# Reading matmul columns in turn from two stretches of SBUF, with one pass of 512 columns for the high weights

## The chip, the core and the metric

The kernel runs on one core of one Trainium2 chip. A core has five engines with queues of their own: TensorE (matrix products, PE in the profile; its weight loads are shown apart as PEld), VectorE (DVE), ScalarE (ACT), GpSimd (POOL) and SyncE (SP, here only issuing DMAs). TensorE reads its operands from SBUF and writes sums to PSUM, which VectorE and ScalarE read. SBUF and PSUM have 128 partitions; a PSUM bank holds 512 float32 values per partition. The metric is the device time of one execution in microseconds, the median of several runs. A product's operands are the stationary one (the weights of the array, 128 by 128, brought by a weight load) and the moving one, whose columns stream through the array.

## The reference

A two-layer trunk over 256 tokens of width 2048. Each layer is a mixer and a gated feed-forward network, each behind an RMS norm and added to its input; the mixer is differential attention in layer 0 and a gated delta rule (a recurrent layer) in layer 1.

```python
def conv_ffn(h, w_up, conv_w, conv_b, w_down):
    u = causal_dwconv(h @ w_up, conv_w) + conv_b
    val, gate = jnp.split(u, 2, axis=-1)
    return (jax.nn.silu(gate) * val) @ w_down

def reference(x, ...):
    for i in range(DEPTH):
        h = rms_norm(x, mixer_norm[i])
        if i % N_MIXERS == 0:
            x = x + diff_attention(h, ...)
        else:
            x = x + gated_deltanet(h, ...)
        x = x + conv_ffn(rms_norm(x, ffn_norm[i]), ...)
    return x
```

All inputs are float32. Nearly all the work is `h @ w` with large weights: query, key and value projections and the output projection of the attention, the input, gate and output projections of the recurrent layer, and up and down projections (2048 to 11008, 5504 to 2048) of both feed-forward networks.

## The kernel before

Activations stand transposed: a row tile holds 128 of the 2048 features on the partitions and the 256 tokens (`T`) along the free axis. A product in full float32 is replaced by three in the faster type fp32r. Each operand is split into a high part (rounded to fp32r) and a low part (the rest), and high times high, low times high and high times low are summed. A row tile of activations holds both parts side by side: `a[:, 0, :]` is the high part (256 columns), `a[:, 1, :]` the low part.

`weights` (line 77) streams a weight chunk of four row tiles by 256 outputs, 512 KB, from HBM into `raw` on SyncE's queue (line 87); ScalarE rounds it to `whi` (line 88) and VectorE subtracts to give `wlo` (line 89). Each of the three has three buffers. The places of `whi` and `wlo` in their buffers are shifted by a number of columns that the caller gives (`place`, `dist`), so that they start at chosen distances, modulo 128 columns, from the activations.

`dense` (line 100) multiplies such chunks with the activations as the moving operand. For each row tile `k` and each of two groups `c` of 128 outputs it issues lines 115, 116 and 117, 256 columns each, into the first half of PSUM bank `c` of `ps`: high weights with high activations, low weights with high activations, high weights with low activations. `dense_tok` (line 125) does the value projection and the gate projection of the recurrent layer the other way round: activations are the stationary operand and 512 columns of weights move (lines 137 to 139). `ps` has two buffers of two banks, so that one block's sums can be read while the next block is multiplied; the other four banks are for small products.

After a block, `merge` (line 121) multiplies the sums by the inverse norm of each token on VectorE (line 123) and writes them to SBUF; it is used by the up projection, by queries and keys and by the recurrent layer's input projection, 134 times in all. Output projections go through `project` (line 237) and `add_out` (line 228), or the recurrent layer's `out` (line 659), which add the sums to the residual stream `x` (line 231, and line 247 in the last block, where the output's DMA follows). In the recurrent layer the gate columns go through `gates` (line 704).

Small products, norms and the recurrent layer's own steps are generators that `tick` (line 72) advances one step after each weight chunk, so that they stand between the large products on TensorE. They are plain float32 products, and sums of squares over partitions by fp32r products with a matrix of ones (line 225). The order of instructions on each engine is fixed when the program is built.

The order of the large products is: queries and keys, values, attention's output projection, the up and down projections, then per block of heads of the recurrent layer its input projections with the gate projection between them and the preceding block's output projection behind them, and at last the second up and down projections.

Of the kernel before, what the change touches and what calls it, by code (L numbers as in the profile page):

```python
# [8 lines left out]
F32 = mybir.dt.float32  # L9
F32R = mybir.dt.float32r  # L10
AF = mybir.ActivationFunctionType
ALU = mybir.AluOpType
# [4 lines left out]
P = 128  # L17
T = 256
D = 2048
KD = D // P  # L20
# [6 lines left out]
class Trunk:  # L27
# [72 lines left out]
    def dense(self, w, kt, acts, place, tiles=2, lead=0, dist=(45, 45)):  # L100
# [4 lines left out]
        for k0, nk in self.chunks(kt, CK, lead):  # L105
            hi, lo = self.weights(w[:, k0:k0 + nk, :], [(place - x) % P for x in dist])
            steps = [(k, c) for k in range(nk) for c in range(tiles)]
            if k0 + nk == kt:
                steps = [(k, c) for c in range(tiles) for k in range(nk)]
            for k, c in steps:  # L110
                a = acts(k0 + k)
                first, last = k0 + k == 0, k0 + k == kt - 1
                s = slice(c * P, (c + 1) * P)
                o = ps[:, c, :T]
                nc.tensor.matmul(o, hi[:, k, s], a[:, 0, :], start=first, stop=False)  # L115
                nc.tensor.matmul(o, lo[:, k, s], a[:, 0, :], start=False, stop=False)  # L116
                nc.tensor.matmul(o, hi[:, k, s], a[:, 1, :], start=False, stop=last)  # L117
            self.tick()
        return ps

    def merge(self, ps, u):

        self.nc.vector.tensor_tensor(u, ps[:, :, :T], self.rstd.unsqueeze(1).to_broadcast([P, 2, T]), ALU.mult)  # L123

    def dense_tok(self, w, kt, acts, dist):
# [4 lines left out]
        for k0, nk in self.chunks(kt, CK // 2):  # L130
            hi, lo = self.weights(w[:, k0:k0 + nk, :], 2 * ((HP + dist) % P,))
            for k in range(nk):
                a = acts(k0 + k)
                first, last = k0 + k == 0, k0 + k == kt - 1
                for c in range(2):
                    ah, al = (a[:, i, c * P:(c + 1) * P] for i in range(2))
                    nc.tensor.matmul(ps[:, c, :], ah, hi[:, k, :], start=first, stop=False)  # L137
                    nc.tensor.matmul(ps[:, c, :], ah, lo[:, k, :], start=False, stop=False)  # L138
                    nc.tensor.matmul(ps[:, c, :], al, hi[:, k, :], start=False, stop=last)  # L139
# [87 lines left out]

    def add_out(self, blk, ps, done):

        x = self.x[:, 2 * blk:2 * blk + 2, :]  # L230
        self.nc.vector.tensor_tensor(x, ps[:, :, :T], x, ALU.add)
# [5 lines left out]
    def project(self, w, kt, acts, place, done, final=False):  # L237

        n = KD // 2
        for b in range(n):  # L240
# [4 lines left out]
            for c in range(2):  # L245
                k = 2 * b + c
                self.nc.vector.tensor_tensor(self.x[:, k, :], ps[:, c, :T], self.x[:, k, :], ALU.add)
# [456 lines left out]
    def gates(self, gd, pg, nv, gp, ident, triu, res):  # L704
# [7 lines left out]
        nc.vector.tensor_tensor(lin, pg[:, 0, :T], self.rstd, ALU.mult)  # L712
# [45 lines left out]
NH = 8  # L758
# [11 lines left out]
def _layout(inputs):  # L770
# [30 lines left out]
    for t, n in ((0, P), (1, T)):  # L801
# [9 lines left out]
        for i in range(2)]  # L811
    out = {
# [3 lines left out]
        "w_v": blocks(x["diff_w_qkv"][0], KD, [[(2 * NH * T + T * h, 2 * T)] for h in range(0, NH, 2)]),  # L816
# [8 lines left out]
        "w_z": blocks(wi, KD, gz),  # L825
# [77 lines left out]
```

## Time and profile before

| | |
|---|---|
| median of 3 runs | 2648.79 us (2647.02 to 2650.22) |
| the profiled execution, first to last instruction | 2646.8 us |
| mean granted TensorE clock | 0.999 |
| weight DMAs (the queue's total) | 475.58 MB in 134064 packets |
| mean DMA traffic | 182 GB/s |

In the profile, a row of a group gives the source line, the engine, the operation, the names `out<-in`, the shapes, the count, then busy time in us and the mean of one in ns, then the time that the engine stood idle just before them and what ended it. Rows of the timeline give start and length in us, and the count of equal instructions merged. Matrix products overlap: the time from one start to the next, not the length of a row, is what each takes of TensorE. A plain float32 product appears as two records, an fp32r product as one.

Stages by the time in which their weights are loaded: attention up to 402 us, first up projection to 871, first down projection to 1105, recurrent layer to 1940, second up projection to 2409, second down projection to the end.

### The profile page before, as it was taken

The page shows a single profiled execution, that of the slowest core. Times are in us where ns is not written, and L with a number is a line of the kernel's source. Part 1 is how long each engine was busy: PE and PEld are TensorE (multiplying, and loading weights), DVE is VectorE, ACT ScalarE, POOL GpSimd, SP SyncE. Part 2 cuts the span into 40 slices and gives each one's busy share as a digit, 9 for nine tenths or more (in the row PEclk, how much of TensorE's full clock was granted, in tenths as well). Part 3 has the DMA queues.
Part 4 walks back from the last instruction along what each step waited for, and adds up shares of the span by engine and source line. Part 5 has one row for each costly group of instructions (what it writes and reads, how often), then busy time and mean ns, then how long its engine had stood idle before and what let it go on. Part 6 is the DMA issues. An engine that isn't in the chain of part 4 may idle for free.

```text
span 2646.8 us, 53675 instructions
## 1 busy us (share of the span) xinstructions
PE 2630.0 (99%) x22352; PEld 2568.2 (97%) x22352; DVE 1843.3 (70%) x2719; ACT 1452.6 (55%) x1994; POOL 112.9 (4%) x221
## 2 busy tenths in 40 slices
PE   8999999999999999999999999999999999999999
PEld 8998899999999999999989989989999999999999
DVE  7776567777777555589787788688677777775444
ACT  6655555555555444485674674574555555554333
POOL 0000000000000000021011021021000000000000
PEclk9999999999999999999999999999999999999999
DMA  5555566665656666555455455455455666666665
GB/s 201 173 176 167 166 192 194 193 196 193 194 195 193 196 192 195 186 161 188 132 167 168 150 168 169 152 169 174 152 194 193 196 193 193 195 194 197 202 201 166
DMA packets 135460, 481.62 MB, mean 182 GB/s; under 512 B 15408, under 2 KB 18480, under 8 KB 135216
## 3 DMA queue, kind: packets, MB, share of 16 engines
q1 hardware_dynamic: 134064, 475.58, 56.5%
q8 instruction: 175, 2.87, 0.4%
q10 hardware_dynamic: 1152, 2.61, 0.3%
q14 instruction: 69, 0.57, 0.1%
HBM read 476.03 MB, written 2.10 MB: 181 GB/s over the span
## 4 chain that ended last, share of the span: by engine, by line
PE 94%; ACT 2%; DVE 2%; issue 1%; DMA 1%; POOL 0%; SPq 0%; DVEq 0%; ACTq 0%
PE ps L115 27%; PE ps L117 27%; PE ps L116 27%; PE ps L138 3%; PE ps L139 3%; PE ps L137 3%; PE mp L607 2%; DVE wlo L89 1%; ACT whi L88 1%; PE mp L225 1%; DVE cv L206 0%; DMA raw<-w_in 0%; PE mp L577 0%; PE mp L571 0%; ACT L454 0%
## 5 line engine op out<-in xcount | busy, mean ns | idle before, releaser
L89 DVE TENSOR_TENSOR wlo<-raw,whi 128x1024 fp32r<-128x1024 f32 (+2 forms) x909 | 1105.6, 1217 | 640.9 <-ACT whi L88 638.6
L88 ACT CAST whi<-raw 128x1024 fp32r<-128x1024 f32 (+2 forms) x909 | 948.1, 1044 | 999.4 <-PE ps L117 835.4
L115 PE MATMUL ps<-h,whi 128*128 128x256 f32 x4304 | 1192.5, 277 | 9.0 <-ACT h L151 5.7
L116 PE MATMUL ps<-h,wlo 128*128 128x256 f32 x4304 | 1192.3, 277 | 3.1 <-DVE wlo L89 3.1
L117 PE MATMUL ps<-h,whi 128*128 128x256 f32 x4304 | 1192.2, 277 | 0.0
L115 PEld LDWEIGHTS ps<-h,whi 128*128 128x128 f32 x4304 | 809.3, 188 | 11.2 <-ACT h L151 5.7
L116 PEld LDWEIGHTS ps<-h,wlo 128*128 128x128 f32 x4304 | 809.8, 188 | 5.6 <-DVE wlo L89 4.0
L117 PEld LDWEIGHTS ps<-h,whi 128*128 128x128 f32 x4304 | 809.8, 188 | 0.7
L115 PE MATMUL ps<-ac,whi 128*128 128x256 f32 x1632 | 450.4, 276 | 0.0
L116 PE MATMUL ps<-ac,wlo 128*128 128x256 f32 x1632 | 450.3, 276 | 0.0
L117 PE MATMUL ps<-ac,whi 128*128 128x256 f32 x1632 | 450.2, 276 | 0.0
L115 PEld LDWEIGHTS ps<-ac,whi 128*128 128x128 f32 x1632 | 306.2, 188 | 0.0
L116 PEld LDWEIGHTS ps<-ac,wlo 128*128 128x128 f32 x1632 | 306.2, 188 | 0.0
L117 PEld LDWEIGHTS ps<-ac,whi 128*128 128x128 f32 x1632 | 306.2, 188 | 0.0
L137 PE MATMUL ps<-whi,h 128*128 128x512 f32 x384 | 150.1, 391 | 0.0
L138 PE MATMUL ps<-wlo,h 128*128 128x512 f32 x384 | 149.7, 390 | 0.2
L139 PE MATMUL ps<-whi,h 128*128 128x512 f32 x384 | 149.2, 388 | 0.0
L115 PE MATMUL ps<-oc,whi 128*128 128x256 f32 x512 | 143.1, 280 | 0.0
L117 PE MATMUL ps<-oc,whi 128*128 128x256 f32 x512 | 142.9, 279 | 0.0
L116 PE MATMUL ps<-oc,wlo 128*128 128x256 f32 x512 | 142.8, 279 | 0.0
L206 DVE SCALAR_TENSOR_TENSOR cv<-u,fcols,cv 128x255 f32<-128x255 f32 (+1 forms) x344 | 142.8, 477 | 0.0
L123 DVE TENSOR_TENSOR u<-ps,rstd 128x512 f32<-128x512 f32 x118 | 81.4, 690 | 38.4 <-PE ps L117 37.7
(202 smaller groups left out, 2180.2 us busy)
## 6 DMA issues: line engine op xcount, KB each, us to landing
raw<-w_up SPq DMA_DIRECT2D x344, 512.0 KB, 4.3
raw<-w_down SPq DMA_DIRECT2D x160, 512.0 KB, 4.1
raw<-w_in SPq DMA_DIRECT2D x128, 512.0 KB, 4.3
raw<-w_z SPq DMA_DIRECT2D x64, 512.0 KB, 3.7
raw<-w_out SPq DMA_DIRECT2D x64, 512.0 KB, 3.6
raw<-w_qk SPq DMA_DIRECT2D x63, 512.0 KB, 4.1
raw<-w_v SPq DMA_DIRECT2D x32, 512.0 KB, 3.6
raw<-w_o SPq DMA_DIRECT2D x32, 512.0 KB, 4.4
```

What stands on the lines that cost most here:

```text
L88: nc.scalar.copy(hi, raw)
L89: nc.vector.tensor_tensor(lo, raw, hi.bitcast(F32), ALU.subtract)
L115: nc.tensor.matmul(o, hi[:, k, s], a[:, 0, :], start=first, stop=False)
L116: nc.tensor.matmul(o, lo[:, k, s], a[:, 0, :], start=False, stop=False)
L117: nc.tensor.matmul(o, hi[:, k, s], a[:, 1, :], start=False, stop=last)
L123: self.nc.vector.tensor_tensor(u, ps[:, :, :T], self.rstd.unsqueeze(1).to_broadcast([P, 2, T]), ALU.mult)
L137: nc.tensor.matmul(ps[:, c, :], ah, hi[:, k, :], start=first, stop=False)
L138: nc.tensor.matmul(ps[:, c, :], ah, lo[:, k, :], start=False, stop=False)
L139: nc.tensor.matmul(ps[:, c, :], al, hi[:, k, :], start=False, stop=last)
L206: nc.vector.scalar_tensor_tensor(out[:, j:], u[:, :T - j], taps[n - 1 - j], out[:, j:], ALU.mult, ALU.add)
L225: last = self.nc.tensor.matmul(out, self.onesr, p[:, j], start=i + j == 0, stop=i + j == n)
L607: nc.tensor.matmul(p[:, v, :], l(v), r[:, v, :], start=i == 0, stop=i == len(terms) - 1)
```

## The change

Moving operands are read in another order. `turns` gives a view of a stretch of columns in which the first and the second half are read in turn: column 0, column 128, column 1, column 129 and so on. In `dense`, the high weights now run over the high and low activations in one pass of 512 columns, which fills a whole PSUM bank (sums of the high part in the first half, of the low part in the second); the low weights run over the high activations and are added to the first half. In `dense_tok` the three products stay, and the weights' columns are read in turn; the arrays `w_v` and `w_z` are permuted on the host, so that their sums come out in natural order. In `dense` the sums come out interleaved, and their readers undo it: `halves` gives the two halves of a bank in natural order. `merge` copies the second half to SBUF on ScalarE, adds it to the first half on VectorE and multiplies by the norm; the residual addition becomes two additions, one for each half (`add_x`). The sums of `gates` go through `merge` too.

```diff
-                o = ps[:, c, :T]
-                nc.tensor.matmul(o, hi[:, k, s], a[:, 0, :], start=first, stop=False)
-                nc.tensor.matmul(o, lo[:, k, s], a[:, 0, :], start=False, stop=False)
-                nc.tensor.matmul(o, hi[:, k, s], a[:, 1, :], start=False, stop=last)
+                nc.tensor.matmul(ps[:, c, :], hi[:, k, s], self.turns(a), start=first, stop=False)
+                nc.tensor.matmul(ps[:, c, :T], lo[:, k, s], self.turns(a[:, :1, :]), start=False, stop=last)
...
+    def turns(self, a):
+
+        return a.rearrange("p i (q j) -> p i j q", q=2)
+
+    def halves(self, ps):
+
+        return [ps[:, :, i * T:(i + 1) * T].rearrange("p c (j q) -> p c q j", q=2) for i in range(2)]
+
     def merge(self, ps, u):
-        self.nc.vector.tensor_tensor(u, ps[:, :, :T], self.rstd.unsqueeze(1).to_broadcast([P, 2, T]), ALU.mult)
+        nc = self.nc
+        n = u.shape[1]
+        main, small = self.halves(ps[:, :n])
+        t = self.sp.tile([P, 2, T], F32, tag="mt", name="mt", bufs=1)[:, :n]
+        v = "p c (q j) -> p c q j"
+        nc.scalar.copy(t.rearrange(v, q=2), small)
+        nc.vector.tensor_tensor(u.rearrange(v, q=2), main, t.rearrange(v, q=2), ALU.add)
+        nc.vector.tensor_tensor(u, u, self.rstd.unsqueeze(1).to_broadcast([P, n, T]), ALU.mult)
...
-                    nc.tensor.matmul(ps[:, c, :], ah, hi[:, k, :], start=first, stop=False)
-                    nc.tensor.matmul(ps[:, c, :], ah, lo[:, k, :], start=False, stop=False)
-                    nc.tensor.matmul(ps[:, c, :], al, hi[:, k, :], start=False, stop=last)
+                    wh, wl = self.turns(hi[:, k:k + 1, :]), self.turns(lo[:, k:k + 1, :])
+                    nc.tensor.matmul(ps[:, c, :], ah, wh, start=first, stop=False)
+                    nc.tensor.matmul(ps[:, c, :], ah, wl, start=False, stop=False)
+                    nc.tensor.matmul(ps[:, c, :], al, wh, start=False, stop=last)
...
+    def add_x(self, k, n, ps):
+        x = self.x[:, k:k + n, :].rearrange("p c (q j) -> p c q j", q=2)
+        for part in self.halves(ps):
+            self.nc.vector.tensor_tensor(x, part, x, ALU.add)
+
     def add_out(self, blk, ps, done):
-        x = self.x[:, 2 * blk:2 * blk + 2, :]
-        self.nc.vector.tensor_tensor(x, ps[:, :, :T], x, ALU.add)
+        self.add_x(2 * blk, 2, ps)
...
-        nc.vector.tensor_tensor(lin, pg[:, 0, :T], self.rstd, ALU.mult)
+        self.merge(pg, lin.unsqueeze(1))
...
+    def turned(w):
+        return w.reshape(*w.shape[:-1], T, 2).swapaxes(-1, -2).reshape(w.shape)
```

More of the change, by code (lines that the diff above doesn't have):

```diff
@@ L824, in _layout @@
         "w_in": blocks(wi, KD, gin),
[L825 removed]
+        "w_z": turned(blocks(wi, KD, gz)),
         "w_out": go.reshape(NB * (D // T), P, 2 * HB, T),
```

4 lines of the change are left out of this document (2 added, 2 removed).

## The prediction

> **What bounds the kernel now.** I read the page first: busy times, chain, costliest groups.
>
> ```profile
> span 2646.8 us, 53675 instructions
> PE 2630.0 (99%) x22352; PEld 2568.2 (97%) x22352; DVE 1843.3 (70%) x2719; ACT 1452.6 (55%) x1994; POOL 112.9 (4%) x221
> PE 94%; ACT 2%; DVE 2%; issue 1%; DMA 1%; POOL 0%; SPq 0%; DVEq 0%; ACTq 0%
> L115 PE MATMUL ps<-h,whi 128*128 128x256 f32 x4304 | 1192.5, 277 | 9.0 <-ACT h L151 5.7
> L115 PE MATMUL ps<-ac,whi 128*128 128x256 f32 x1632 | 450.4, 276 | 0.0
> L115 PE MATMUL ps<-oc,whi 128*128 128x256 f32 x512 | 143.1, 280 | 0.0
> L137 PE MATMUL ps<-whi,h 128*128 128x512 f32 x384 | 150.1, 391 | 0.0
> ```
>
> TensorE's own stream is 94% of the chain and hardly ever idle. The mean of one product (277 ns) is a latency of overlapping products; what one costs is the step from start to start. The view by stretches gives it where nothing but lines 115 to 117 runs (500 to 800 us), and shows the stages; columns are length, then busy time and count of each engine, granted clock, DMA share, GB/s.
>
> ```profile
> core 0: us, PE busy (x) PEld busy (x) DVE busy (x) ACT busy (x) POOL busy (x), PEclk, DMA share, GB/s
> 500.00:800.00 300.00, 300.00 (x2650) 300.00 (x2649) 214.90 (x306) 163.66 (x222) 0.00 (x0) 1.00 0.60 194
> 403.00:872.00 469.00, 469.00 (x4139) 468.95 (x4138) 335.04 (x477) 257.29 (x349) 0.00 (x0) 1.00 0.61 194
> 1107.00:1420.00 313.00, 311.64 (x2440) 292.04 (x2440) 266.41 (x481) 205.57 (x284) 50.42 (x103) 1.00 0.53 168
> 1420.00:1834.00 414.00, 413.29 (x3569) 391.86 (x3569) 326.75 (x538) 245.43 (x336) 59.97 (x112) 1.00 0.51 163
> 1200.00:1210.00 10.00, 10.00 (x45) 8.26 (x44) 9.55 (x22) 5.64 (x7) 0.00 (x0) 1.00 0.67 208
> ```
>
> 300 us / 2650 = 113.2 ns per product of 256 columns, at a granted clock of 1.00. Next the timeline of TensorE, for products of 512 columns, plain fp32 products of 256 (line 372), and the small fp32r products of line 225.
>
> ```profile
> 255.62 0.39 PE L138 MATMUL ps<-wlo,h 128*128 128x512 f32 x1
> ...
> 265.40 0.39 PE L139 MATMUL ps<-whi,h 128*128 128x512 f32 x1
> 265.62 0.59 PE L372 MATMUL mp<-aT,v 128*128 128x256 f32 x2
> 266.05 0.38 PE L373 MATMUL mp<-aT,v 128*128 128x128 f32 x2
> 266.27 0.38 PE L372 MATMUL mp<-aT,v 128*128 128x256 f32 x1
> ...
> 273.37 0.64 PE L225 MATMUL mp<-sqp,onesr 128*128 128x256 f32 x4
> 273.84 0.39 PE L138 MATMUL ps<-wlo,h 128*128 128x512 f32 x1
> ```
>
> From 255.62 to 265.40 stand 44 products, so 43 steps: 9.78/43 = 227.4 ns for 512 columns. That is twice 113.2 to within 0.5%, with one weight load in either. So the step is set by columns (0.442 ns each) and holds no visible price per product or per load. A plain fp32 record of 256 columns takes (266.05 - 265.62)/2 = 215 ns, 0.84 ns a column: less than twice 0.442. So the array can go a little faster than the fast products go; at half the column rate some 5% of loss is gone. I read this as a limit on how fast contiguous four-byte columns reach the array, since a slower array clock would have stretched both kinds alike. This reading carries the forecast.
>
> **The change, part by part.** Lines 115 to 117 run 4304 + 1632 + 512 = 6448 times, one set for each row tile and 128 outputs, so now cost 3 x 113.2 = 339.6 ns a set. Lines 137 to 139 run 3 x 384 = 1152 products.
>
> *Joining the two passes of the high weights.* Three loads become two; columns stay 768 a set. As the step is set by columns, this alone is worth nothing: bounds 0 and, if a hidden price of 2 ns sat in each product (rounding of the two steps above), 6448 x 2 ns = 13 us. I take 0. The load of the next high weights must now fit beside the 256-column pass; it did fit within 113.2 ns, so this can hold that pass at 113 ns and no higher.
>
> *Columns in turn from two stretches 128 columns apart.* No row shows such a read; every moving operand is contiguous now. If it lifts the limit, a fast column costs half a plain fp32 column: 512 columns 215 ns, 256 columns 107.5 ns, or up to 113 if the load holds it. I take 215 + 109 = 324 ns. A set then saves 339.6 - 324 = 15.6 ns, times 6448 = 101 us; lines 137 to 139 save (227.4 - 215) x 1152 = 14 us. Together 115 us. Lower bound on the saving: none (the limit stays), or a loss (rivals). Upper bound: line 373 takes (266.27 - 266.05)/2 = 110 ns for 128 columns, twice which is 5 more than 215; so 5 ns of a plain fp32 record may be a price per product, which the fast ones don't show. Without it 512 columns take 210 and 256 take 105: savings of 24.6 ns x 6448 + 17.4 ns x 1152 = 179 us. The starts are given to 0.01 us, an error as large as these 5 ns, so I put the bound halfway, 147 us.
>
> *More work to read the sums.* Rows by line:
>
> ```profile
> L123 DVE TENSOR_TENSOR u<-ps,rstd 128x512 f32<-128x512 f32 x118 | 81.4, 690 | 38.4 <-PE ps L117 37.7
> L123 DVE TENSOR_TENSOR qkr<-ps,rstd 128x512 f32<-128x512 f32 x16 | 11.0, 689 | 1.3 <-PE ps L117 0.6
> L231 DVE TENSOR_TENSOR x<-ps,x 128x512 f32<-128x512 f32 x55 | 37.8, 687 | 23.5 <-PE ps L117 23.3
> L612 ACT COPY w<-mp 128x512 f32<-128x512 f32 x8 | 4.7, 588 | 13.6 <-PE mp L607 13.6
> L88 ACT CAST whi<-raw 128x1024 fp32r<-128x1024 f32 x887 | 931.0, 1051 | 963.3 <-PE ps L117 803.2 <-PE ps L139 65.8 <-ACT cv L204 50.3
> ```
>
> Each of the 134 merges (118 + 16, and a narrow one for the gates) gains a ScalarE copy (588 ns, line 612) and a VectorE addition (690 ns): 79 and 92 us in all. Each of 55 residual additions becomes two: 38 us. The readers now step over every second PSUM element; no row prices that. Bounds: nothing, or double (each such instruction 0.69 us more). I take nothing: the nearest rows are lines 123 and 231, which read as many PSUM elements and already go over two banks.
>
> Is it covered? A feed-forward block in the stage 403 to 872 holds 335.04/43 = 7.79 us of VectorE and 257.29/43 = 5.98 us of ScalarE in 10.9 us. After: 8.48 and 6.57 in 32 x 324 ns = 10.37 us, so 82% and 63%; with doubled reads 9.17 us, 88%, still under. The merge's addition waits for its copy, and the copy may stand behind one weight cast (1051 ns); behind the addition on VectorE stand the next low-weight subtraction and the convolution. ScalarE's casts wait mostly for TensorE to free a buffer (803.2 us): the weights are ahead by the three buffers, so about 2 us of delay inside a block stays hidden. The sums have two buffers, and the next block covers ten microseconds.
>
> In the first recurrent block (1107 to 1420) it is tight: VectorE 266.41 of 313 us and, around the inversion, 9.55 of 10. Fifteen merges fall there (10 us more VectorE), and TensorE's own time falls by about 13 us. 277 of 300 us is 92% as a mean, so I charge these 10 us in full as exposed; in the later blocks (326.75 of 414) nothing. At the end, the last addition comes twice:
>
> ```profile
> 2642.99 0.42 DVE x L247
> 2643.42 0.33 DVEq L899
> ```
>
> which adds 0.42 us, and at the start the first wide pass needs the low half of the activations as well, about 0.5 us. Costs: 11 us.
>
> **Sum.** 2646.8 - 115 + 11 = 2542.8 us of span. The runs' median, 2648.79, lies 2.0 us above the profiled span, which I keep: 2545 us.
>
> **The rivals.**
>
> *R1, the limit is per column in any order.* Then the turned read changes nothing, joining passes gives nothing, and the 11 us of costs remain: 2648.8 + 11 = 2660; with VectorE well covered, 2650. For it: the loss is so exactly proportional to columns that it could belong to fast products as such, fed from anywhere. Against: the plain fp32 row. This is the case in which the change doesn't do what it says.
>
> *R2, changing stretch at every column halves the reader.* One mechanism: if the reader fetches a group of neighbouring columns at once and holds only one group, each turned column needs its own fetch. It decides as soon as a fetch costs more than one column's time. Price: the plain fp32 pace, 0.84 ns a column: a set 645 ns (430 + 215), 305 more, times 6448 = 1969 us, and 1152 x (430 - 227) = 234 us: 2648.8 + 2203 = about 4850 us. Against it: nothing in the rows; a contiguous read never tests it. The Trainium skill, page SBUF — State Buffer, section Specifications, says that lines are 16 bytes and that full bandwidth needs at least two hits per line, each move to a new line paying. By that rule turned columns hit each line once before leaving it, and R2 would hold; no run here shows it, and contiguous columns, with four hits per line, already lose.
>
> *R3, the gain is taken back by collisions of two reads.* The code places weights and activations at chosen distances (arguments 45, 27, 15), so the relative place of weight load and moving columns matters. Line 225, which is not placed so, takes (273.84 - 273.37)/4 = 117.5 ns, 4.3 more than 113.2. The turned read walks both stretches at half speed while the distances stay as they were. If that costs 4.3 ns per 256 columns everywhere: (3 x 6448 + 2 x 1152) x 4.3 = 93 us, and the gain shrinks to 115 - 93 - 11 = 11: 2638 us.
>
> **How the numbers follow.** Chances: forecast 0.64, R1 0.16, R2 0.12, R3 0.08. A measurement of this kernel tells about 0.2% (5 us) from no change. The forecast and R3 are faster: 0.72. R1 splits into within 0.2% (0.05) and slower (0.11); R2 is slower: 0.12, so 0.23. The forecast's own range runs from 2648.8 - 147 = 2502 (costs hidden) to 2590 (the load holding the short pass at 113 ns, 26 us, and some 19 us from doubled PSUM reads in the recurrent blocks). The range goes from there over R3 and R1 to 2665 and leaves out R2 and the far tail.
>
> **What would show it.** In the feed-forward stage each set should step 322 to 328 ns, the wide pass 215 and the short one 108 to 113, and products of lines 137 to 139 about 215; TensorE idle as now. Under R1 227 and 113 stand; under R2 near 430 and 215; under R3 steps between, differing by line with the placement. Idle time of TensorE behind the low weights between 1107 and 1420 would show VectorE as the bound. The forecast is wrong if the wide pass still steps 227.

## The result, and the profile after

The changed kernel takes 2613.5 us (median of 4 runs, 2612.4 to 2618.3) against 2649.4 us before (4 runs): a ratio of 0.9872, interval 0.9858 to 0.9886. It is 36 us faster. The forecast was 104 us faster (2545), so the direction was right and the size was not, by 68 us.

First the page of the changed kernel: span, busy times, TensorE's granted clock in 40 slices, the chain that ended last, and four of the costliest groups.

```profile
span 2611.1 us, 41169 instructions
PE 2557.8 (98%) x15904; PEld 2328.6 (89%) x15904; DVE 1945.4 (75%) x2911; ACT 1510.2 (58%) x2119; POOL 107.2 (4%) x221
PEclk9999999999999999999989999999799999999999
PE 95%; ACT 2%; DVE 1%; DMA 1%; issue 1%; SPq 0%; ACTq 0%; DVEq 0%
L114 PE MATMUL ps<-h,whi 128*128 128x512 f32 x4304 | 1427.0, 385 | 19.1 <-ACT zt L704 9.7
L115 PE MATMUL ps<-h,wlo 128*128 128x256 f32 x4304 | 1182.7, 275 | 2.2 <-DVE wlo L89 2.2
L245 DVE TENSOR_TENSOR x<-ps,x 128x512 f32<-128x512 f32 (+1 forms) x114 | 77.0, 676 | 16.5 <-PE ps L115 15.4
L136 DVE TENSOR_TENSOR u<-u,rstd 128x512 f32<-128x512 f32 x118 | 81.7, 692 | 3.3
```

Products fell from 22352 to 15904, which is the 6448 joined passes. VectorE gained 102 us and ScalarE 58. TensorE is 98% busy and not 99%, and its clock, full in all slices before, has two slices below 9. The residual additions (L245) now step over every second PSUM element. The 110 of them of full size take 685 ns where contiguous ones took 687; the 676 of the row takes in four of half the size.

Next the stretches of the changed kernel: one inside the first up projection, where only the dense products run, and then the recurrent layer in five stretches. That layer begins at 1053 us, its last block ends at 1919, and the inner marks are where its four bursts of token-major products (L151 to L153) begin. The last two rows lie inside the third of the five.

```profile
500.00:800.00 300.00, 300.00 (x1834) 275.89 (x1833) 238.31 (x343) 184.58 (x258) 0.00 (x0) 1.00 0.60 201
...
1053.00:1127.00 74.00, 73.31 (x449) 66.65 (x448) 58.71 (x109) 50.68 (x74) 7.50 (x16) 1.00 0.58 188
1127.00:1270.00 143.00, 142.07 (x988) 127.03 (x987) 122.00 (x208) 87.59 (x120) 26.18 (x46) 1.00 0.56 178
1270.00:1500.00 230.00, 216.16 (x1458) 194.63 (x1457) 180.43 (x310) 136.16 (x196) 23.74 (x53) 0.96 0.45 145
1500.00:1702.00 202.00, 198.76 (x1345) 179.68 (x1343) 167.91 (x281) 119.97 (x165) 26.05 (x53) 0.98 0.52 169
1702.00:1919.00 217.00, 197.95 (x1262) 177.04 (x1262) 161.79 (x281) 118.02 (x174) 23.52 (x50) 0.91 0.41 135
...
1343.00:1356.00 13.00, 8.78 (x28) 7.26 (x29) 7.43 (x19) 4.41 (x7) 2.30 (x8) 0.51 0.00 1
1356.00:1366.00 10.00, 10.00 (x63) 9.22 (x62) 8.46 (x16) 4.68 (x5) 0.00 (x0) 1.00 0.41 131
```

The same five stretches of the kernel before:

```profile
1094.00:1174.00 80.00, 78.79 (x668) 77.47 (x667) 61.34 (x118) 57.48 (x83) 17.51 (x30) 1.00 0.53 169
1174.00:1337.00 163.00, 162.85 (x1361) 152.63 (x1361) 136.75 (x241) 104.47 (x148) 21.39 (x49) 1.00 0.50 157
1337.00:1546.00 209.00, 208.60 (x1759) 198.16 (x1758) 165.02 (x273) 127.04 (x176) 31.07 (x59) 1.00 0.51 163
1546.00:1752.00 206.00, 205.69 (x1744) 195.12 (x1743) 161.06 (x268) 124.16 (x168) 28.49 (x53) 1.00 0.51 164
1752.00:1929.00 177.00, 177.00 (x1516) 167.72 (x1515) 141.05 (x230) 94.21 (x131) 14.28 (x28) 1.00 0.51 169
```

In the up projection 1834 products are 917 sets, 300 / 917 = 327 ns each; from start to start in the trace it is 327.5 (218.3 for the wide pass, 109.2 for the short one), of 339.6 before. That is what the change was for, and it is there. The table has every stage, each from the first load of its weights to that of the next; here and below stage times are differences of two starts in the trace, us.

| stage | before | after | difference |
|---|---|---|---|
| attention: qk, v, o projections | 389.4 | 374.5 | -14.9 |
| first up and down projection | 703.4 | 677.5 | -25.9 |
| recurrent layer | 835.1 | 865.7 | +30.6 |
| second up and down projection | 716.8 | 691.9 | -24.9 |

Outside the recurrent layer the change gains 66 us. Inside it 31 go again, though the sets and the token-major products are shorter there too. The two lists of stretches show where: the first two gain 26 us together (217 of 243), the fourth 4, the third loses 21, the last 40. In those two TensorE stands idle 14 and 19 us and its mean clock is 0.96 and 0.91. Over the layer its records show half clock for 65 us, in pieces of 3.4 to 17 us; before there were none.

The timeline of TensorE in the third stretch has one such place (columns: start, duration, engine, line, operation, and in brackets the idle time before it and what ended it).

```profile
1340.31 0.36 PE L492 MATMUL mp<-grow,sel 128*128 128x256 f32 x1 [1.00 <-DVE d L495]
1343.98 0.77 PE L514 MATMUL mp<-cv 128*128 128x128 f32 x2 [3.32 <-DVE cv L507]
...
1346.68 1.06 PE L604 MATMUL mp<-con,cv 128*128 128x128 f32 x4
1350.98 0.79 PE L114 MATMUL ps<-h,whi 128*128 128x512 f32 x1 [3.24 <-ACT zt L704]
```

Small products of the recurrence (L492, L514, L515, L604) stand next to each other with no dense product between them. TensorE waits for VectorE and then for ScalarE, in these rows twice more than 3 us, and around these gaps it goes at half clock (0.51 in the window from 1343 to 1356, 1.00 in the next): the wide pass at 1350.98 takes 0.79 us as a record where the mean is 0.385. What put the small products there, and why VectorE is late, is what the experiments below take apart.

### The profile page after: what moved, and what is told of

Same layout as the page of the kernel before. It is cut to its first block, busy times and chain, and to the rows that moved or that the text cites. A ratio compares the mean times of both kernels' runs of the same rounds, so it can differ in the third digit from the quotient of the medians.

```text
span 2611.1 us, 41169 instructions
## 1 busy us (share of the span) xinstructions
PE 2557.8 (98%) x15904; PEld 2328.6 (89%) x15904; DVE 1945.4 (75%) x2911; ACT 1510.2 (58%) x2119; POOL 107.2 (4%) x221
## 3 DMA queue, kind: packets, MB, share of 16 engines
q10 hardware_dynamic: 1152, 2.61, 0.3%
## 4 chain that ended last, share of the span: by engine, by line
PE 95%; ACT 2%; DVE 1%; DMA 1%; issue 1%; SPq 0%; ACTq 0%; DVEq 0%
PE ps L114 54%; PE ps L115 27%; PE ps L151 3%; PE ps L153 3%; PE ps L152 3%; PE mp L625 2%; PE mp L239 1%; PE mp L515 1%; ACT whi L88 0%; DMA raw<-w_in 0%; PE mp L595 0%; PE mp L589 0%; DVE wlo L89 0%; PE mp L604 0%; DMA raw<-w_qk 0%
## 5 line engine op out<-in xcount | busy, mean ns | idle before, releaser
L89 DVE TENSOR_TENSOR wlo<-raw,whi 128x1024 fp32r<-128x1024 f32 (+2 forms) x909 | 1104.2, 1215 | 535.4 <-ACT whi L88 521.8
L114 PE MATMUL ps<-h,whi 128*128 128x512 f32 x4304 | 1427.0, 385 | 19.1 <-ACT zt L704 9.7
L115 PE MATMUL ps<-h,wlo 128*128 128x256 f32 x4304 | 1182.7, 275 | 2.2 <-DVE wlo L89 2.2
L114 PEld LDWEIGHTS ps<-h,whi 128*128 128x128 f32 x4304 | 818.8, 190 | 135.0 <-ACT zt L704 10.8
L115 PEld LDWEIGHTS ps<-h,wlo 128*128 128x128 f32 x4304 | 831.4, 193 | 5.1 <-DVE wlo L89 3.6
L114 PE MATMUL ps<-ac,whi 128*128 128x512 f32 x1632 | 535.1, 382 | 0.0
L115 PE MATMUL ps<-ac,wlo 128*128 128x256 f32 x1632 | 444.8, 273 | 0.0
L114 PEld LDWEIGHTS ps<-ac,whi 128*128 128x128 f32 x1632 | 308.4, 189 | 43.1 <-issue 0.2
L115 PEld LDWEIGHTS ps<-ac,wlo 128*128 128x128 f32 x1632 | 313.3, 192 | 0.1
L114 PE MATMUL ps<-oc,whi 128*128 128x512 f32 x512 | 171.0, 387 | 0.9 <-DVE oc L673 0.9
L151 PE MATMUL ps<-whi,h 128*128 128x512 f32 x384 | 146.2, 381 | 0.9 <-ACT whi L88 0.9
L153 PE MATMUL ps<-whi,h 128*128 128x512 f32 x384 | 145.9, 380 | 0.0
L115 PE MATMUL ps<-oc,wlo 128*128 128x256 f32 x512 | 141.1, 276 | 0.0
L114 PEld LDWEIGHTS ps<-oc,whi 128*128 128x128 f32 x512 | 98.2, 192 | 15.1 <-DVE oc L673 1.3
L115 PEld LDWEIGHTS ps<-oc,wlo 128*128 128x128 f32 x512 | 99.5, 194 | 0.1
L218 ACT ACTIVATE cv<-u,fcols 128x256 f32<-128x256 f32 x172 | 93.9, 593 | 0.6 <-DVE u L136 0.5
L245 DVE TENSOR_TENSOR x<-ps,x 128x512 f32<-128x512 f32 (+1 forms) x114 | 77.0, 676 | 16.5 <-PE ps L115 15.4
L220 DVE SCALAR_TENSOR_TENSOR cv<-u,cols,cv 128x255 f32<-128x255 f32 (+2 forms) x192 | 84.5, 477 | 1.9 <-ACT cv L216 1.8
L136 DVE TENSOR_TENSOR u<-u,rstd 128x512 f32<-128x512 f32 x118 | 81.7, 692 | 3.3
```

Of the source, the lines that this page charges most:

```text
L89: nc.vector.tensor_tensor(lo, raw, hi.bitcast(F32), ALU.subtract)
L114: nc.tensor.matmul(ps[:, c, :], hi[:, k, s], self.turns(a), start=first, stop=False)
L115: nc.tensor.matmul(ps[:, c, :T], lo[:, k, s], self.turns(a[:, :1, :]), start=False, stop=last)
L136: nc.vector.tensor_tensor(u, u, self.rstd.unsqueeze(1).to_broadcast([P, n, T]), ALU.mult)
L151: nc.tensor.matmul(ps[:, c, :], ah, wh, start=first, stop=False)
L153: nc.tensor.matmul(ps[:, c, :], al, wh, start=False, stop=last)
```

## The experiments

### One part at a time

*turn_only* keeps three passes and turns the columns of each; there is one read of the sums.

```diff
-                nc.tensor.matmul(ps[:, c, :], hi[:, k, s], self.turns(a), start=first, stop=False)
-                nc.tensor.matmul(ps[:, c, :T], lo[:, k, s], self.turns(a[:, :1, :]), start=False, stop=last)
+                o = ps[:, c, :T]
+                ah, al = self.turns(a[:, 0:1, :]), self.turns(a[:, 1:2, :])
+                nc.tensor.matmul(o, hi[:, k, s], ah, start=first, stop=False)
+                nc.tensor.matmul(o, lo[:, k, s], ah, start=False, stop=False)
+                nc.tensor.matmul(o, hi[:, k, s], al, start=False, stop=last)
```

> Three passes of 256 columns as before, but every large product reads its moving columns in turn; one VectorE read of the sums, as before. Theory A (the gain is all in the turned read, the loss of the changed kernel is in what joining brought into the recurrent layer): a set of three steps 3 x 109.2 = 327.6 ns, a 512-column product 216 to 219; the recurrent layer, 835 us before and 866 us in the changed kernel, takes about 809; total 2649 - 80 - 10 = about 2559 us. Rival B (faster large products alone uncover the recurrent layer's own latencies): the recurrent layer stays near 866 and the total near 2613. Rival C (the passes are faster only where joined): 113 ns a pass, total 2640 to 2650.

*join_only* keeps the joined pass and reads all columns in order (w_v and w_z not permuted).

```diff
     def turns(self, a):
-        return a.rearrange("p i (q j) -> p i j q", q=2)
+        return a
```

> One pass of 512 columns for the high weights, all columns contiguous; copies and additions as in the changed kernel. Theory A: 227 + 113 = 340 ns a set, feed-forward up stages 468 us as before, and a recurrent layer that loses as in the changed kernel (some 40 to 57 us over its product time): total 2680 to 2705 us. Rival C (joining brings the rate): 328 ns a set, total near 2613. Rival B: with slow products nothing is uncovered, the recurrent layer stays near 835 and the total near 2655.

Measured: turn_only 2602.1 us (ratio 0.9834, 0.9819 to 0.9848), 44 us faster than before and 11 faster than the whole change. join_only 2771.0 us (1.047, 1.0454 to 1.0486). The same stretch of the up projection, turn_only first, then join_only:

```profile
500.00:800.00 300.00, 300.00 (x2689) 300.00 (x2688) 216.81 (x309) 165.91 (x225) 0.00 (x0) 1.00 0.66 197
```

```profile
500.00:800.00 300.00, 300.00 (x1733) 262.10 (x1732) 227.60 (x325) 173.68 (x245) 0.00 (x0) 1.00 0.59 190
```

A turned pass of 256 columns steps 111.7 ns from start to start (300 / 2689 = 111.6), and not the 109.2 expected, so no total that was expected for turn_only is met. A set is 335, 4.6 less than before: 6448 x 4.6 + 1152 x 12.4 = 44 us, which is the whole gain of this kernel. In join_only a set takes 347 ns from start to start (230.9 + 115.8), 7 more than three separate passes, and 353 in the second up projection. So joining is worth about nothing only in the forecast: with contiguous columns it costs, with turned ones it gains 335 - 327.5 = 7.5 ns a set. In the recurrent layer turn_only takes 819.8 us, 15 less than before: turning alone loses nothing there. join_only takes 907.6 us there, 72 more than before, of which its longer sets are 11 to 21 (1552 sets in that layer, 7 to 14 ns each). So the loss in that layer comes with joining, whether columns are turned or not.

### What a column costs, and what a pass

*probe* is the kernel before with a pattern of its own in each block of the up and down projections: the columns in q stretches, d columns apart, taken in turn; in the second up projection with the joined pass.

```diff
+    def turn(self, a, q, d):
+        if d == 0:
+            return a
+        return a.rearrange("p (g q j) -> p g j q", q=q, j=d)
```

> Steps of the large products by the way in which columns are read. The kernel before with its three passes, but the first up projection changes its reading order every five blocks: contiguous; two stretches 128, 64, 32, 16, 8, 4, 2 columns apart; four stretches 64 apart. The second up projection uses the joined form: contiguous; 128 apart; 256 apart with 128 for the low weights; 64; 32; high turned and low contiguous; high contiguous and low turned; four stretches; eight. The first down projection (turned) and the second (contiguous) change the place of the weights every block. The sums stay in the order of reading and the second half of a joined bank is not read, so these terms are left out. Theory E (any second stretch lifts the limit): 113 contiguous, 109 for all distances down to 4. Rival F (the two reads must lie in other 64-byte pieces): 109 at 16 and above, 113 at 8 and below. Rival G (a full round of the weights' placement matters): steps that follow the place of the weights by 4 ns and more, turned or not. For the joined pass: 218.4 at 128 as in the changed kernel, 216 at 256 as for the products that move weights.

Windows of *probe*, three passes: two stretches 128, 4 and 2 columns apart, then four stretches 64 apart. After these, joined sets: contiguous; 128 apart; only the wide pass turned. (A window of some 40 us counts two or three products that only overlap its edges; steps in the text are from start to start. *probe* and *widths* ran once each, for these steps alone.)

```profile
458.00:508.00 50.00, 50.00 (x451) 50.00 (x450) 36.86 (x53) 27.74 (x40) 0.00 (x0) 1.00 0.63 196
726.00:776.00 50.00, 50.00 (x451) 50.00 (x450) 36.85 (x53) 27.63 (x40) 0.00 (x0) 1.00 0.58 198
790.00:830.00 40.00, 40.00 (x355) 40.00 (x354) 29.02 (x43) 22.14 (x31) 0.00 (x0) 1.00 0.60 194
834.00:870.00 36.00, 36.00 (x266) 36.00 (x265) 21.62 (x31) 16.42 (x24) 0.00 (x0) 1.00 0.52 165
...
1965.00:1995.00 30.00, 30.00 (x172) 26.38 (x171) 20.58 (x30) 15.76 (x21) 0.00 (x0) 1.00 0.59 184
2010.00:2045.00 35.00, 35.00 (x215) 32.21 (x215) 26.00 (x38) 19.75 (x28) 0.00 (x0) 1.00 0.60 201
2210.00:2255.00 45.00, 45.00 (x270) 41.34 (x269) 32.28 (x46) 24.70 (x34) 0.00 (x0) 1.00 0.56 196
```

| columns | 256 alone, ns | joined set, ns (wide + short) |
|---|---|---|
| contiguous | 113.3 | 353.3 (231.8 + 121.5) |
| two stretches, 128 to 4 apart | 111.7 | 327.5 (218.3 + 109.2), 32 to 256 apart |
| two stretches, 2 apart | 113.3 | not run |
| wide pass turned, short one contiguous | | 335.6 (215.8 + 119.8) |
| wide pass contiguous, short one turned | | 340.0 (231.7 + 108.3) |
| four stretches | 136.7 | 390.0 (278.2 + 111.8) |

Two columns apart, a turned pair lies within 16 bytes, and there is no gain; from four columns (16 bytes) apart there is all of it. Two stretches in turn help; four lose. The down projections of the same kernel vary where the weights lie against the activations. Turned, all eight placements step 111.66 to 111.67 ns; contiguous, they step 113.4 to 123.3. So the place of the weights costs a contiguous read up to 10 ns and a turned read nothing; I take it for a collision with the weight load, which no run shows apart. By the same reading the joined contiguous passes of join_only stand in a bad place, a worse one in its second feed-forward stage (353 ns) than in its first (347); other places were not tried for them.

*widths* is the kernel before with all three passes of the up projections at one width per five blocks, turned in the first and contiguous in the second.

```diff
+                    n = max(wide, T) if first else wide
+                    x = a.rearrange("p i t -> p (i t)")[:, :n]
+                    if turned:
+                        x = x.rearrange("p (q j) -> p j q", q=2)
```

> The kernel before, but in both up projections the three products of a set run over 64, 128, 192, 224, 256, 288, 320, 384 or 512 columns, changing every five blocks (the first row tile of a block over at least 256); first stage turned, second contiguous. Widths below 256 leave columns out, the others read more of the same. Theory H (a weight load holds 111.7 ns and sets the step of a turned pass of 256): turned 111.7 at all widths up to 256, then about 121, 135, 162 and 216. Rival I (a fixed price of about 5 ns a product): turned 33, 60, 86, 98, 112, 125, 138, 165, 218. Contiguous above 256: 0.442 ns a column plus what the place of the weights adds: 128, 142, 170, 227 or more.

Its windows for 64, 128, 224, 256, 288 and 384 turned columns:

```profile
420.00:490.00 70.00, 70.00 (x330) 70.00 (x329) 27.28 (x40) 21.81 (x29) 0.00 (x0) 0.50 0.32 105
510.00:590.00 80.00, 80.00 (x377) 80.00 (x376) 32.09 (x44) 22.97 (x32) 0.00 (x0) 0.50 0.31 100
...
660.00:708.00 48.00, 48.00 (x432) 48.00 (x432) 34.88 (x51) 26.27 (x37) 0.00 (x0) 1.00 0.62 197
715.00:760.00 45.00, 45.00 (x405) 45.00 (x404) 32.09 (x47) 25.01 (x34) 0.00 (x0) 1.00 0.63 197
770.00:820.00 50.00, 50.00 (x410) 50.00 (x409) 33.39 (x46) 24.79 (x35) 0.00 (x0) 1.00 0.57 180
895.00:960.00 65.00, 65.00 (x402) 65.00 (x401) 32.78 (x46) 24.80 (x34) 0.00 (x0) 1.00 0.42 138
```

From 192 to 256 columns a product steps 111.7 ns whatever its width, as theory H expected, then 122.5 at 288, 135.8 at 320, 162.5 at 384 and 215.8 at 512. These widths lie on one line, 0.417 ns a column and 2.5 ns, which meets 111.7 near 260 columns: above it the columns set the step, below it a floor for each product that does not depend on them. At half clock the floor is 213.3 ns, for 64 and 128 columns alike, so it goes with TensorE's clock. I take it for the weight load, of which each product has one. No run here shows that: the load rows are busy all the time at 288 and 384 columns too, where the columns set the step. Contiguous passes follow the same floor (112 at 192 and 224 columns) and above it cost more: 133.3, 148.4 and 180.0 at 288, 320 and 384. Before the change, 113.2 ns was a column price just above this floor.

### The recurrent layer: the reads

*one_read* is the changed kernel with the second read of the sums taken out: the copy and the addition in `merge` and the second residual addition.

```diff
-        nc.scalar.copy(t.rearrange(v, q=2), small)
-        nc.vector.tensor_tensor(u.rearrange(v, q=2), main, t.rearrange(v, q=2), ALU.add)
-        nc.vector.tensor_tensor(u, u, self.rstd.unsqueeze(1).to_broadcast([P, n, T]), ALU.mult)
+        r = self.rstd.rearrange("p (q j) -> p q j", q=2).unsqueeze(1).to_broadcast([P, n, 2, P])
+        nc.vector.tensor_tensor(u.rearrange(v, q=2), main, r, ALU.mult)
```

> The changed kernel, but the sums of high weights with low activations are computed and never read: this leaves out one of the three terms, with its ScalarE copies and its second VectorE additions. Rival D (the recurrent layer of the changed kernel is late because VectorE and ScalarE have more to do): its 57 us come back, total about 2557. Theory A in the form that the fixed order of the small steps costs the time: most of it stays where small steps stand in rows with no large product between them (the last block above all), total 2575 to 2600.

*mix* is a full version: three turned passes and one read in the recurrent layer, joined and turned elsewhere.

```diff
+                if not self.joined:
+                    ...
+                    continue
...
+            self.joined = False
...
+            self.joined = True
```

> The changed kernel, with three turned passes and one read of the sums in the recurrent layer alone. Theory A: attention and feed-forward as in the changed kernel, the recurrent layer about 809 instead of 866 us, total about 2556 us. Rival B: the recurrent layer near 866, total near 2613.

*mix_reads* is mix with the third pass of the recurrent layer written to the second half of the bank, so that the sums are read twice as in the changed kernel.

```diff
-                    nc.tensor.matmul(o, hi[:, k, s], al, start=False, stop=last)
+                    nc.tensor.matmul(ps[:, c, T:], hi[:, k, s], al, start=False, stop=last)
```

> As mix (recurrent layer with three turned passes), but there the low activations' pass goes to the second half of the bank, and the sums are read twice, with the copy and the additions of the changed kernel. Rival D (the copies and additions cost the time): the recurrent layer, 823 us in mix and 866 in the changed kernel, rises to 840 or more, total 2590 or more. Theory A in the form that the fixed order of the small steps costs it: the extra reads alone cost under 8 us there, total 2571 to 2579.

*mix_out* is mix with the last projection of the recurrent layer (w_out) joined too.

```diff
+                    self.joined = True
...
+                    self.joined = False
```

> As mix, but the output projection of the recurrent layer is joined too (512 sets at 327.5 instead of 335 ns: 3.8 us). If joining as such is harmless where the small steps keep large products between them: total 2567 us, 4 below mix. If any joined product in that layer brings the loss back: 2580 or more.

Measured: one_read 2592.5 us (0.9797, 0.9782 to 0.9812); mix 2570.8 (0.9716, 0.97 to 0.9732); mix_reads 2579.2 (0.974, 0.9725 to 0.9754); mix_out 2574.6 (0.9723, 0.9707 to 0.9739). The recurrent layers take 846.9, 822.7, 832.9 and 825.0 us. So mix gains everything that the change gains outside the layer, and 12 us inside it, where the change loses 31. It is 43 us faster than the changed kernel and the fastest full version here; mix_out is the same within the noise. The 809 us that were expected for the layer of mix again took a turned pass at 109.2 ns. mix_out was to gain 4 us on mix or lose 9 and more, and does neither, so it decides little. The last three stretches of mix:

```profile
1288.00:1493.00 205.00, 204.78 (x1770) 196.18 (x1769) 165.01 (x282) 126.75 (x178) 31.91 (x56) 1.00 0.53 165
1493.00:1702.00 209.00, 204.44 (x1757) 194.66 (x1757) 164.46 (x276) 128.24 (x178) 28.89 (x61) 1.00 0.52 163
1702.00:1876.00 174.00, 173.89 (x1523) 166.52 (x1522) 140.58 (x231) 94.67 (x132) 14.14 (x28) 1.00 0.55 172
```

With the reads taken out of the changed kernel its layer is 19 us shorter (865.7 to 846.9); with them put into mix it is 10 longer, between the two outcomes expected. But one_read is still 24 us behind mix, with the same work on VectorE and ScalarE in that layer, and its clock stands at half for 48 us. The reads are not all of it.

### The recurrent layer: the order

The order of TensorE's instructions is fixed when a kernel is built. Set side by side, before and turn_only, whose passes have the same shapes, have the same order, with dense products between the small steps of the recurrence. The changed kernel and join_only, with joined passes, share another: at the end of three blocks, and through almost all of the last, the small steps stand in rows with no dense product between. The longest such row of the changed kernel has 276 records and spans 33.6 us; in the kernel before the longest spans 2.7. mix has dense products there. one_read has an order of its own, with its longest row, 33.1 us, in the last block too. Three kernels fix the order of TensorE's products. They leave the order on VectorE and ScalarE to the build, and in the traces it comes out differently in each, so what is called the price of the order or of the reads below holds with what the build made of these engines.

*pinned* is the changed kernel with each group of small steps held behind the last dense product issued before it in the code, and the next dense product behind the small steps.

```diff
+        with self.tc.issue_after(self.big):
+            self.steps()
...
+                if self.pinned and self.small is not None:
+                    self.tc.add_manual_dep(f.ins, self.small.name, NOSYNC)
```

> The changed kernel with the same instructions; only TensorE's order in the recurrent layer is fixed to the order in which the code issues them, with a chunk of large products between any two steps of the small ones. If the loss there comes from the order (small steps in rows with nothing large between, TensorE idle and its clock halved behind): the recurrent layer falls from 866 us to 815 to 830, no stretch at half clock, total 2560 to 2578. If it comes from the work of copies and additions or from the faster products as such: it stays at 845 or more, total 2590 or more.

*same_order* is the changed kernel with TensorE's products of the recurrent layer in the order of mix; *same_order_one* does that to one_read. (`ORDER` is that order, listed.)

```diff
+            rank = [k for a, n in ORDER for k in range(a, a + n)]
+            for a, b in zip(rank, rank[1:]):
+                self.tc.add_manual_dep(items[b][0], items[a][-1].name, NOSYNC)
```

> The changed kernel, instruction for instruction; in the recurrent layer TensorE's products are queued in the order that the build gave to mix, so that a joined set stands where mix has its three passes. If the loss of joining there is the order that the build makes for it: the recurrent layer takes 811 to 825 us instead of 866, with no stretch at half clock, total 2556 to 2572. If it is the copies and additions: 840 or more, total 2588 or more. If faster products as such uncover the small steps: 850 or more.

> As same_order, but the sums of high weights with low activations are computed and never read (one of the three terms is left out, with its copies and additions). If the order is the cause, about 811 us in the recurrent layer (mix's 823 less 1552 sets at 7.5 ns), total 2552 to 2560; against same_order it gives the price of the extra reads under one and the same order of products, between 0 and 10 us.

Measured: pinned 2720.3 us (1.0278, 1.0261 to 1.0296), the layer 970.2: the other way from what was expected. The order of the code puts the steps of the block inversion behind each other where nothing hides them, as the waits of TensorE in *pinned* show (what waits, for what: us in all, times, longest):

```profile
PE mp L591 <- DVE tcc L572: 56.6, 4, 15.0
```

It is a worse order, so it tells nothing of what is wrong with the build's, but it shows the range: 849 to 970 us with identical instructions. same_order takes 2595.7 us (0.9806, 0.979 to 0.9822), the layer 849.4, which is the outcome expected if copies and additions cost it, though 16 us below the changed kernel; same_order_one 2571.1 (0.9714, 0.97 to 0.9729), the layer 823.6 where 811 was expected. The last three stretches of same_order, 21 us of the first of them, two waits of its TensorE in the layer, and the same stretches of same_order_one:

```profile
1289.00:1513.00 224.00, 207.83 (x1384) 185.07 (x1383) 175.68 (x303) 137.31 (x195) 26.28 (x63) 0.98 0.49 153
1513.00:1727.00 214.00, 204.04 (x1373) 183.38 (x1372) 173.21 (x290) 132.06 (x184) 27.51 (x54) 0.98 0.50 156
1727.00:1902.00 175.00, 171.14 (x1192) 153.84 (x1192) 147.78 (x243) 97.50 (x134) 14.18 (x28) 1.00 0.54 169
...
1385.00:1406.00 21.00, 13.41 (x97) 11.79 (x97) 20.22 (x34) 6.96 (x7) 2.10 (x6) 0.94 0.59 194
```

```profile
PE mp L571 <- DVE tcc L552: 9.6, 3, 7.0
PE ps L116 <- DVE wlo L90: 6.5, 5, 3.0
```

```profile
1289.00:1496.00 207.00, 203.27 (x1382) 183.48 (x1381) 165.15 (x283) 127.06 (x180) 33.18 (x59) 0.99 0.53 163
1496.00:1705.00 209.00, 202.97 (x1369) 181.61 (x1368) 162.31 (x274) 127.05 (x176) 25.25 (x58) 0.99 0.51 162
1705.00:1877.00 172.00, 169.80 (x1187) 152.87 (x1186) 138.25 (x227) 94.17 (x132) 13.97 (x28) 1.00 0.53 172
```

The last stretch is 217 us in the build's order and 175 in mix's, with the reads in both: that stretch is the order's. The first two go the other way (217 and 236 us): the build's order takes dense products early that are missing as cover at the end, so the net price is 865.7 - 849.4 = 16 us. The third stretch is 224 us with the reads and 207 without, in one order of TensorE: that one is the reads'. There TensorE waits 7 us for VectorE's part of the block inversion (tcc), which comes late behind residual additions and low weights: VectorE is busy 20.2 of the 21 us up to there. Elsewhere it waits for the low weights (wlo).

| recurrent layer, us | one read | two reads |
|---|---|---|
| three passes, order of mix | 822.7 | 832.9 (own order) |
| joined, order of mix | 823.6 | 849.4 |
| joined, the build's order | 846.9 | 865.7 |

In the last column the order of TensorE costs 16 us; in the middle row the reads cost 26, where 0 to 10 were expected. The 23 us of the first column and the 19 of the last row go through one_read, whose build made an order of its own, so the 19 are not the reads alone. The first column shows a third thing: joined sets, 7.5 ns shorter, should save 1552 x 7.5 = 12 us in the layer and save nothing. Over the last three stretches TensorE's busy time falls by 7 us from mix to same_order_one (583.1 to 576.0), in the same 588 us. What it gains it waits; the largest wait of TensorE in that layer, first in same_order_one, then in mix, is for the low weights:

```profile
PE ps L116 <- DVE wlo L90: 8.8, 6, 3.4
```

```profile
PE ps L120 <- DVE wlo L89: 3.0, 6, 0.7
```

## Why the prediction was right, and where it failed

**Contiguous columns as the bound: right.** Turned columns go at 0.417 ns each and contiguous ones at 0.44. The wide pass steps 218.3 ns (forecast 215), and L151 to L153 215 to 219 (215). R1 is out: under it the wide pass would have stepped 227.

**R2: out.** Turned columns 4 to 128 apart lose nothing. Two columns apart, they step as contiguous ones. By the Trainium skill, page SBUF — State Buffer, section Specifications, each move to a new 16-byte line pays unless a line is hit at least twice before; the wide pass moves at every column and steps 218.3 ns, less than the 227 of contiguous columns, so the measurement decides against it for two lines in turn. Four stretches in turn (278 ns) do pay.

**R3: the wrong way round.** The place of the weights matters, up to 10 ns a product, but for contiguous reads; turned reads do not feel it. That it is a collision of two reads stays a reading.

**The set: 327.5 ns, not 324.** The prediction took 215 + 109 and gave the load as a possible cap of 113 on the short pass. From start to start the short pass does step 109.2, and the 3.5 ns lie on the wide one (218.3). But the set is also the sum of what turned products of 512 and of 256 columns step alone (215.8 + 111.7), and I take the floor of 111.7 for the cause. Which of the two passes it holds is not shown, as starts shift when widths change: where *widths* goes from 192 to 256 columns and back, one step is 139 ns and a later one 85, all others 111 or 112. Outside the recurrent layer are 4896 of the sets: 4896 x 3.5 = 17 us, which is all of what the gain there fell short by (66 us measured, about 80 forecast).

**Joining "alone is worth nothing": mis-sized, in both directions.** It makes two products of three, and with turned columns a product of 256 stands on the floor of 111.7, so it gains 7.5 ns a set; with contiguous columns it loses 7 to 14, I take it by the placement. The forecast of the set, 324 ns, came out near by luck: joining and turning were summed as 768 columns at one price, not as passes with a floor.

**The failed step** is the one that ends "so I charge these 10 us in full as exposed; in the later blocks (326.75 of 414) nothing". 54 of the 68 us lie in it and in the gain counted beside it: the layer was to take 835.1 - 24.2 (sets) - 9.5 (token-major products) + 10 = 811, and took 865.7. Point by point, from the 801 us that it would be without the charge:

| step | layer, us | shown by |
|---|---|---|
| forecast without the charge | 801 | |
| shorter sets and products not realised | 823.6 | same_order_one |
| reads (charged: 10) | 849.4 | same_order |
| the build's order (charged: 0) | 865.7 | the changed kernel |

Taken the other way round, over one_read, the shares of reads and order differ, as said above.

The price was wrong, and the place in part. The 480th and 481st weight chunks stand on the two sides of the first long row of small products. Their low weights (L89), in the kernel before and then in the changed one:

```profile
L89 DVE TENSOR_TENSOR wlo<-raw,whi x2: 1228/1228/1229, 1387.4 to 1389.0; 128x1024 fp32r<-128x1024 f32 x2
```

```profile
L89 DVE TENSOR_TENSOR wlo<-raw,whi x2: 1226/1226/1227, 1331.1 to 1357.2; 128x1024 fp32r<-128x1024 f32 x2
```

They start 1.6 us apart before and 26 after, and 1387 us lies in the time from 1107 to 1420 that the prediction took as tight. The largest loss, 40 us in the last block, lies behind the 1834 us at which its windows end: chunks 636 and 637 start there at 1899 and 1901 us before, at 1843 and 1881 in the changed kernel. There, in the changed kernel, VectorE is far from full:

```profile
1835.00:1875.00 40.00, 32.65 (x343) 29.54 (x342) 19.18 (x31) 12.75 (x22) 7.01 (x11) 0.70 0.16 55
```

So two things were missed. A mean load (326.75 of 414, 79%) does not show that VectorE is full for the 21 us around one inversion, as in same_order; and where small steps stand in a row, TensorE waits for their chain through the engines, at half clock behind it, whatever their load. The sign that the prediction named, TensorE idle behind the low weights, is 2.2 us in the whole changed kernel (L115 on its page above). Nor did the prediction ask who decides the order: I kept the order of before and shortened it, though joined passes are other instructions, for which the build made another order. Of the 22 us not realised, 5 are the 3.5 ns that a set is longer (1552 of them) and 12 the joining; for the remaining 5 no run tells more. That the joined sets' gain goes into waits for the low weights is read from the waits; no kernel with earlier low weights was run.

**Strided reads of PSUM at no cost: right** (685 ns against 687). The 7.8 us of VectorE in a 10.9 us feed-forward block did leave room: outside the recurrent layer nothing was lost to the reads (one_read's feed-forward stages are within 1 us of the changed kernel's).

## What to carry to other kernels

Ask of each pass which floor it stands on (its columns, or a price per product), and sum floors, not columns: a remedy for one floor shows only until the next, and the worth of one edit can depend on another (joining costs 7 ns a set with contiguous columns and gains 7.5 with turned ones). Where long products hide a chain of small steps, making fewer of them can change the order that a build chooses; look at the stretch with the longest wait in the chain, not at the mean load of a stage. An edit that pays in uniform stages can be left out of the one stage that pays for it, as mix does.

## What the runs showed of the hardware

- Four-byte columns taken in turn from two stretches at least 16 bytes apart step faster than contiguous ones: 215.8 ns for a product of 512 against 227 to 233; from four stretches 278, from eight 520. The Trainium skill, page TensorE: Matmul & The Clock Gate, section "Wait — 56ns, not 53.3ns?", gives N / 2.4 GHz + 2.5 ns; the turned widths agree (122.5 ns at 288, 215.8 at 512), the contiguous ones do not.
- Products of this type, each with a load of 128 x 128 weights of its own, step no less than 111.7 ns at full clock in rows of one width (192 to 256 turned columns) and 213.3 at half clock (64 and 128). Only a short pass behind a wide one was seen below it from start to start (109.2 and 108.3), where only the sum of the set is sure.
- Around idle gaps of 2 to 3.7 us the granted clock of the changed kernel fell to half for 3.4 to 17 us. It was also at half in *widths* with 64 and 128 columns (windows 420 to 590 above), where TensorE's rows show no idle time at all: a product steps 213 ns there, 1.9 times as long as one of 224 columns. The Trainium skill, page TensorE: Matmul & The Clock Gate, section "Part 1: The HAM clock gate", has the clock halve after an idle window of about 3.4 us; the longer gaps agree with it. Whether it covers the 64 columns is open: they are busy rows, but rows overlap, and at 0.417 ns a column 64 columns are 27 ns of array time.
